# Layer 1's MLP: a plain second half that reads its operand from DRAM, and eight products of the first half ahead of the rest

## The chip, the cores and the metric

One Trainium2 chip, one core. The metric is the device time of one execution of the whole program in microseconds (us), the median of several runs. The names of the engines are those of the profile: PE (TensorE, matrix products), DVE (VectorE), ACT (ScalarE), POOL (GpSimd), SP (the queue that issues the transfers).

## What is computed

A backbone of two layers on 1024 latent tokens of width 1024, with 256 context tokens beside them in layer 0. In each layer a mixer (attention) with an output projection is followed by an MLP. The change concerns the end of layer 1, where only the 1024 latent tokens are left:

```
x   = x + g1 * rms_norm(m, norm_g[1, 1])                    # m: output projection of the mixer
h   = modulate(rms_norm(x, norm_g[1, 2]), sh2, sc2)         # 1024 x 1024
f   = square(relu(h @ w_mlp_in[1])) @ w_mlp_out[1]          # 1024 x 4096, then back to 1024 x 1024
out = x + g2 * rms_norm(f, norm_g[1, 3])
```

All data are float32. A product of two float32 matrices is made of three passes: each operand is split into a high part (rounded to the matrix engine's type) and a low part (the rest), and `dense` (L384 to L391) issues high x high, high x low and low x high into one accumulator, on lines L389, L390 and L391.

## The kernel before, in words

**Splitting.** `split` (L193) copies the high part on ACT (L189) or DVE (L191) and subtracts on DVE or POOL (L196). The split operands live in slots of 128 x 1024, handed out by `Slots` (`R`), and named r, s or w in the profile after the pool that they come from. Every weight is loaded through two staging tiles of 512 KB (tag `stg`, `NSTG = 2`, named ws).

**Output projection** (`out_projection`, L1556). Eight tiles of 128 tokens, each 48 matmuls of 128x512. After a tile comes `residual` (gate, add), and one tile later `late`: `norm_T` normalises, transposes on PE (L316), scales into four raw quadrants xq of the tokens (ACT L321, DVE L323), and for tokens of the first half of the sequence splits quadrants at once. For tiles 4 to 7 `Tokens7.after` (L1355) then forms the token combinations in place with four 128x512 operations (L1362 to L1365), on POOL, for tile 7 on DVE.

**First half of the MLP** (`up7`, L1380). The 4096 hidden features are taken in 16 turns of 256. Each turn is a 2x2 block product done with seven block products in place of eight (Strassen's method in Winograd's form): `Seven` (L1312) forms the combinations of the weight blocks on POOL (L1326, tile cm), `Tokens7` those of the tokens. One block product is 4 k-tiles x 3 passes = 12 matmuls of 128x512, so a turn has 84 and the half 1344. Products 1 and 2 use tokens of the first half of the sequence alone and give the first quadrant of the result; products 5, 6, 3, 7 and 4 need tokens of all eight tiles. Products 1, 6, 7 and 4 add up in one accumulator, which is read in between. In the kernel before, the two products of turn 0 that need no later tokens are issued ahead, before the last `late` (`start` = 2, `begun`). Then `Tokens7.split` (L1367) splits the other four token operands, each as two pairs of 128x1024, and the loop runs with weight operands prepared six products ahead. `put` adds, applies relu and square on DVE (L1444, L1445) and stores the result (hr) in a DRAM tensor hT (L1446).

**Second half** (`Down7`, L1462). Also seven products in place of eight. The 32 rows of 128 hidden features are taken in six units of 2, 2, 3, 3, 3 and 3 pairs. `weights` loads two rows of w_mlp_out per pair and forms seven split operands: combinations on POOL (cm, p, L1326), low parts on POOL (L196). `load` fetches a part of hT for 256 tokens (tile hw), and `prep` forms seven combinations of it (ch, L1326) and their split operands (ho, ACT L189 and L196), on DVE, for the last unit on POOL. Each product is then added into the sums acc (DVE L1552; the first ones are copied by ACT, L1550). In all 16 pairs x 4 token pairs x 7 products x 3 passes = 1344 matmuls of 128x512. The first operands are prepared during the last turn of the first half (`freed`, L2068, as each token operand gives back its slots; `last_up`, L2072). In the last unit `finish1` (L2127) does the final norm, gate and residual of each tile of 128 tokens and stores it.

**Order.** The order on each engine and on SP's queue is fixed when the program is compiled, by a scheduler that goes by the order of the source, its own estimate of times, and `tc.high_priority()` where that is given. At run time every engine and SP work in that order.

**A plain product in the same kernel.** Layer 0's MLP (`mlp`, L1217) does both halves without the seven-product method: split operands, `dense`, sums on DVE (L1244).

## Time and profile before

| | us |
|---|---|
| median of 3 runs | 3236.47 (3233.67 to 3236.80) |
| the profiled execution | 3236.59 |
| its span (first to last instruction) | 3234.8 |
| mean granted clock of PE | 0.982 |

The span and all rows below are of the one profiled execution. "PE busy" counts the records of matmuls, which overlap, so a stretch in which PE is busy throughout is read by the distance from one matmul's start to the next. In the table of stretches the columns are the stretch, its length, the busy time of each engine with the number of its instructions, PE's granted clock (1.00 is 2.4 GHz, 0.50 is 1.2 GHz), and the share and rate of the transfers.

### The profile page before, as it was taken

Reading aid. Unit: us, or ns where it says so; the run is one execution under the profiler, and the core shown is the slowest. Engines: PE = TensorE matmul, PEld = TensorE weight load, DVE = VectorE, ACT = ScalarE, POOL = GpSimd, SP = SyncE. Lnnn points to the kernel's source line nnn. Section 1 sums busy time; section 2 is a strip of 40 time slices with the busy share of each in tenths; the row PEclk is TensorE's granted clock in tenths of the full one; section 3 lists DMA queues with packets and bytes.
Section 4 is the critical chain, followed back from the end, with each engine's and each line's share of the span. In section 5 each row is a group of like instructions: output and inputs, shape, how many; then the busy total and the mean of one; then the engine's idle time right before and its main releaser. Section 6 shows DMA issues by size and latency. Waiting matters only on the chain. (4 is left out here: it accounts for less than half of the span.)

```text
span 3234.8 us, 47996 instructions
## 1 busy us (share of the span) xinstructions
PE 3075.3 (95%) x18037; PEld 2538.6 (78%) x18037; DVE 1745.7 (54%) x3361; ACT 1262.9 (39%) x2664; POOL 1252.0 (39%) x1055
## 2 busy tenths in 40 slices
PE   7999999999999999999999999999998999959997
PEld 4778888887887887878888788999886788836775
DVE  4345565798562343343343641157656655568885
ACT  4222577788342111111111341368854333343432
POOL 2356100135452222322323552301346433484778
PEclk8999999999999999999999999999999899989999
DMA  7555212132332222132211354134443333322233
GB/s 251 179 157 160 84 50 60 56 86 92 126 126 91 65 83 79 55 96 66 71 61 37 107 141 114 34 96 117 135 141 103 108 108 110 114 88 85 89 117 114
DMA packets 242240, 327.59 MB, mean 101 GB/s; under 512 B 37496, under 2 KB 166536, under 8 KB 242008
## 3 DMA queue, kind: packets, MB, share of 16 engines
q1 hardware_dynamic: 241784, 324.01, 32.6%
q8 instruction: 142, 2.33, 0.3%
q14 instruction: 90, 0.74, 0.1%
q10 hardware_dynamic: 128, 0.26, 0.0%
q0 software_dynamic: 96, 0.26, 0.0%
HBM read 256.79 MB, written 67.67 MB: 100 GB/s over the span
## 5 line engine op out<-in xcount | busy, mean ns | idle before, releaser
L196 POOL TENSOR_TENSOR r<-ws,r 128x1024 fp32r<-128x1024 f32 (+1 forms) x100 | 231.1, 2323 | 306.3 <-ACT r L189 306.1
L391 PE MATMUL mm<-s,r 128*128 128x512 f32 (+1 forms) x912 | 318.5, 349 | 0.8 <-POOL r L196 0.7
L389 PE MATMUL mm<-s,r 128*128 128x512 f32 (+1 forms) x912 | 318.6, 349 | 0.0
L390 PE MATMUL mm<-s,r 128*128 128x512 f32 (+1 forms) x912 | 318.1, 349 | 0.0
L1244 DVE TENSOR_TENSOR acc<-mm,acc 128x512 f32<-128x512 f32 x300 | 203.7, 687 | 168.1 <-PE mm L391 167.8
L1230 DVE TENSOR_TENSOR hr<-hr 128x512 f32<-128x512 f32 (+1 forms) x96 | 72.6, 756 | 360.6 <-ACT hr L1229 360.6
L189 ACT ACTIVATE r<-ws 128x1024 fp32r<-128x1024 f32 (+1 forms) x107 | 106.8, 999 | 368.7 <-DMA ws<-in_w_mlp_out_dram 190.7
L189 ACT ACTIVATE pt<-tp 128x512 f32<-128x512 f32 (+1 forms) x382 | 204.1, 548 | 47.4 <-PE tp L802 16.6
L389 PE MATMUL mm<-r,r 128*128 128x512 f32 x538 | 213.0, 396 | 1.3 <-DVE r L191 0.9
L391 PE MATMUL mm<-r,r 128*128 128x512 f32 x538 | 210.1, 391 | 0.6 <-POOL r L196 0.6
L390 PE MATMUL mm<-r,r 128*128 128x512 f32 x538 | 209.6, 390 | 0.0
L1229 ACT ACTIVATE hr<-mm 128x512 f32<-128x512 f32 (+1 forms) x96 | 50.2, 523 | 391.1 <-PE mm L391 383.0
L196 POOL TENSOR_TENSOR r<-hr,r 128x512 fp32r<-128x512 f32 (+1 forms) x66 | 84.5, 1280 | 303.9 <-DVE r L191 303.6
L725 ACT ACTIVATE P<-P,nm 128x1280 f32<-128x1280 f32 (+1 forms) x160 | 189.9, 1188 | 18.2 <-DVE P L733 17.3
L391 PEld LDWEIGHTS mm<-s,r 128*128 128x128 f32 x912 | 171.7, 188 | 25.8 <-POOL r L196 1.2
L390 PEld LDWEIGHTS mm<-s,r 128*128 128x128 f32 x912 | 171.8, 188 | 24.8
L389 PEld LDWEIGHTS mm<-s,r 128*128 128x128 f32 x912 | 171.9, 188 | 24.7
L389 PE MATMUL mm<-r,e 128*128 128x512 f32 (+1 forms) x400 | 151.0, 378 | 2.5 <-ACT e L189 1.6
L391 PE MATMUL mm<-r,e 128*128 128x512 f32 (+1 forms) x400 | 150.7, 377 | 1.7 <-POOL e L196 1.0
L390 PE MATMUL mm<-r,e 128*128 128x512 f32 (+1 forms) x400 | 150.3, 376 | 0.2 <-DVE r L196 0.2
L166 POOL TENSOR_SCALAR sbm<-ssb 128x2 f32<-128x2 f32 x20 | 4.0, 199 | 357.7 <-ACT jk L974 357.6
L1326 POOL TENSOR_TENSOR cm<-ws 128x512 f32<-128x512 f32 x46 | 68.5, 1488 | 181.8 <-DMA ws<-in_w_mlp_in_dram 179.2
(367 smaller groups left out, 8785.1 us busy)
## 6 DMA issues: line engine op xcount, KB each, us to landing
wm<-in_w_mod_dram SPq DMA_DIRECT2D x80, 512.0 KB
ws<-in_w_mlp_in_dram SPq DMA_DIRECT2D x64, 512.0 KB
ws<-in_w_mlp_out_dram SPq DMA_DIRECT2D x64, 512.0 KB
q<-qT SPq DMA_DIRECT2D x224, 128.0 KB
ws<-in_w_in_dram SPq DMA_DIRECT2D x36, 512.0 KB
hT<-hr SPq DMA_DIRECT2D x64, 256.0 KB
hw<-hT SPq DMA_DIRECT2D x16, 768.0 KB
xres<-xn SPq DMA_DIRECT2D x18, 512.0 KB
```

Source lines behind the costliest of these rows:

```text
L166: pool.tensor_scalar(m, ss, 1.0 / n, EPS, op0=OP.mult, op1=OP.add)
L189: act.activation(o, i, AF.Copy)
L196: lo_eng.tensor_tensor(lo, src, f(hi), op=OP.subtract)
L389: pe.matmul(pt, sh, mh, start=first and k == 0, stop=False, skip_group_check=free)
L390: pe.matmul(pt, sh, ml, start=False, stop=False, skip_group_check=free)
L391: pe.matmul(pt, sl, mh, start=False, stop=k == n - 1, skip_group_check=free)
L725: act.activation(P, P, AF.Exp, scale=-1.0, bias=self.nm[:, u:u + 1], accum_out=self.sums[:, u:u + 1])
L1229: act.activation(r, pt, AF.Relu)
L1230: dve.tensor_tensor(r, r, r, op=OP.mult)
L1244: dve.tensor_tensor(acc[t][:, s], pt, acc[t][:, s], op=OP.add)
L1326: self.add.tensor_tensor(o, a, b, op=r[1])
```

## The change

Five things change.

1. The second half is a plain product (`Down`): 32 chunks of 128 hidden features, in eleven units of 2 and ten times 3. A chunk is one load of 512 KB of w_mlp_out and one of 512 KB of hT (all 1024 tokens), each split once. For each of 8 token tiles and 2 column halves a unit makes one accumulation of 3 chunks x 3 passes and adds it to acc. That is 32 x 8 x 2 x 3 = 1536 matmuls. Chunks are prepared after the products of the last turn (`freed`), and then after every second token tile.
2. In the first half, products 1 and 2 of turns 0 to 3 (`early` = 4) are issued after the output projection's last tile and before the last `late`. Their weights are loaded for themselves (`prep_early`, 512 KB in rows of 512 bytes). The result of product 1 is kept for each turn (`keep1`), by transfer for turns 2 and 3, and added on DVE to the later sums of these turns.
3. The token operands of products 5, 6, 7 and 4 are split in two goes: for tiles 4 to 6 (384 of 512 tokens) ahead of the last `late`, for tile 7 after it, there with both low parts on DVE.
4. In both layers' output projections the last tile's `residual` and the last `late` are given high priority.
5. One slot of 128 x 1024 is held for `keep1` until turn 3 ends.

```diff
-        def split(self, p):
+        def split(self, p, o, engs):
             raw = self.q[{5: 11, 7: 12, 6: 22, 4: 21}[p]]
             for c, (a, b) in enumerate(self.slots(p)):
-                split(a, b, raw[:, 2 * c:2 * c + 2, :], act, (dve, pool)[c])
+                split(a[:, :, o], b[:, :, o], raw[:, 2 * c:2 * c + 2, o], act, engs[c])
...
-        seq = [(u, p) for u in range(n) for p in (TURN if u else (1, 2, 5, 6, 3, 7, 4))]
+        seq = [(u, p) for u in range(n) for p in (TURN if u >= early else (5, 6, 3, 7, 4))]
...
+        def prep_early(u):
+            w = stg.tile([128, 1024], F32, tag="stg", name="ws", bufs=NSTG).rearrange("p (a n) -> p a n", a=8)
+            sp.dma_start(w, w_mlp_in[l, :, u * 256:u * 256 + 128].rearrange("(a p) f -> p a f", p=128))
+            for kh in range(2):
+                operand((u, kh + 1), w[:, 4 * kh:4 * kh + 4, :], (dve, pool)[kh])
...
-        ready(start)
+        prep_early(0)
         yield
-        ps, st = env["ps"], {}
-        begun = [product(*x) for x in seq[:start]]
+        ps = env["ps"]
+        keep1 = [x for a in rows() for x in a]
+        for u in range(early):
+            b = product(u, 1)
+            own = keep1[u] if u < 2 else env["mid"].tile([128, 512], F32, tag="O", name="O", bufs=2)
+            act.activation(own, b, AF.Copy)
+            if u >= 2:
+                sp.dma_start(keep1[u], own)
+            if u + 1 < early:
+                prep_early(u + 1)
+            b = product(u, 2)
+            r = env["mid"].tile([128, 512], F32, tag="O", name="O", bufs=2)
+            dve.tensor_tensor(r, b, own, op=OP.add)
+            act.activation(r, r, AF.Relu)
+            pool.tensor_tensor(r, r, r, op=OP.mult)
+            store(u, 0, 0, r)
+        for p in (5, 6, 7, 4):
+            X.split(p, slice(0, 384), (dve, pool))
         yield
...
+                if u < early:
+                    dve.tensor_tensor(st[u, name], b, keep1[u], op=OP.add)
+                else:
+                    act.activation(st[u, name], b, AF.Copy)
...
-                put(1, 0, None)
-
-    class Down7:
...
+                put(1, 0, keep1[u] if u < early else None)
+                if u == early - 1:
+                    env["done1"]()
+
+    class Down:
...
+        def load(self, where):
...
+            w = stg.tile([128, 1024], F32, tag="stg", name="ws", bufs=NSTG)
+            sp.dma_start(w, w_mlp_out[self.l, r, :])
+            h = where.tile([128, 1024], F32, tag="hw", name="hw", bufs=3)
+            sp.dma_start(h, self.hT[r, :])
+            self.raw.append((w, h))
+
+        def prep(self, where):
...
+            s = [R.get(1) for _ in range(4)]
+            v = [x.view([128, 1024]) for x in s]
+            split(v[0], v[1], h, act, dve)
+            split(v[2], v[3], w, act, pool)
+            self.ops.append((s, v[:2], v[2:]))
+            self.load(where)
+
+        def run(self, acc, ps, hp, finish, before_last):
+            for ui, m in enumerate(self.units):
...
+                for t in range(8):
+                    o = slice(t * 128, (t + 1) * 128)
+                    for h in range(2):
+                        s = slice(h * 512, (h + 1) * 512)
+                        pt = ps.tile([128, 512], F32, name="mm", tag="mm", bufs=6)
+                        dense(pt, [(x[0][:, o], x[1][:, o]) for _, x, _ in ops],
+                              [(y[0][:, s], y[1][:, s]) for _, _, y in ops])
+                        if ui == 0:
+                            act.activation(acc[t][:, s], pt, AF.Copy)
+                        else:
+                            dve.tensor_tensor(acc[t][:, s], pt, acc[t][:, s], op=OP.add)
+                    if last:
+                        finish(t, acc[t])
+                    elif t % 2 == 1 and len(self.ops) < self.units[ui + 1]:
+                        self.prep(hp)
...
-            residual(pts, G, xt, xn, ps, pool if i < n - RD else dve)
+            with tc.high_priority() if i == n - 1 else ExitStack():
+                residual(pts, G, xt, xn, ps, pool if i < n - RD else dve)
...
-        late()
+        with tc.high_priority():
+            late()
...
-    D1 = Down7(1, UNITS1, 4, hT)
+    D1 = Down(1, (2,) + (3,) * 10, hT)
...
     for p in (5, 6, 7, 4):
-        X3.split(p)
+        X3.split(p, slice(384, 512), (dve, dve))
...
-    D1.weights(7, temp_down)
-    D1.run(acc, ps, tmp, hp[0], temp_down, 4, finish1, last1)
+    D1.run(acc, ps, hp[0], finish1, last1)
```

## Rows read from the trace of the kernel before

**Rows 1.** The page's head and part 1: span, busy time of each engine.

```profile
span 3234.8 us, 47996 instructions
PE 3075.3 (95%) x18037; PEld 2538.6 (78%) x18037; DVE 1745.7 (54%) x3361; ACT 1262.9 (39%) x2664; POOL 1252.0 (39%) x1055
```

**Rows 2.** Table of stretches: layer 1's MLP in five stretches; last, layer 0's MLP.

```profile
2491.00:2528.40 37.40, 16.41 (x40) 11.47 (x41) 32.06 (x27) 14.19 (x23) 30.85 (x20) 0.59 0.12 39
2528.40:2825.10 296.70, 296.70 (x1288) 241.46 (x1287) 170.44 (x216) 100.97 (x177) 102.94 (x67) 1.00 0.34 114
2825.10:2863.00 37.90, 8.97 (x30) 5.36 (x28) 10.31 (x9) 14.12 (x26) 37.61 (x31) 0.64 0.30 90
2863.00:3223.50 360.50, 322.74 (x1316) 250.03 (x1316) 297.09 (x386) 136.65 (x287) 263.77 (x195) 0.97 0.31 99
3223.50:3234.80 11.30, 0.00 (x1) 0.00 (x0) 5.02 (x8) 1.45 (x4) 3.21 (x3) 0.71 0.41 117
...
1260.00:1680.00 420.00, 420.00 (x2031) 336.96 (x2030) 163.74 (x247) 52.13 (x71) 117.38 (x72) 1.00 0.24 74
```

**Rows 3.** Waits of PE from 2825 to 3226 us: in total, times, longest.

```profile
PE b L389 <- ACT ho L189: 29.4, 4, 26.5
PE a L391 <- DVE ho L196: 13.8, 4, 6.6
PE b L391 <- DVE ho L196: 9.6, 6, 2.7
```

**Rows 4.** Timeline of PE in layer 0's MLP: start, duration, instruction.

```profile
1355.80 0.40 PE L389 MATMUL mm<-s,r 128*128 128x512 f32 x1
...
1364.67 0.40 PE L391 MATMUL mm<-s,r 128*128 128x512 f32 x1
...
1372.63 0.39 PE L389 MATMUL mm<-r,r 128*128 128x512 f32 x1
...
1381.24 0.39 PE L391 MATMUL mm<-r,r 128*128 128x512 f32 x1
```

**Rows 5.** Costliest groups of POOL, DVE and ACT in layer 0's MLP.

```profile
L196 POOL TENSOR_TENSOR r<-ws,r 128x1024 fp32r<-128x1024 f32 x52 | 126.3, 2449 | 247.4 <-ACT r L189 247.4
...
L1244 DVE TENSOR_TENSOR acc<-mm,acc 128x512 f32<-128x512 f32 x240 | 163.2, 688 | 144.5 <-PE mm L391 144.2
...
L189 ACT ACTIVATE r<-ws 128x1024 fp32r<-128x1024 f32 x52 | 55.2, 1063 | 283.9 <-DMA ws<-in_w_mlp_out_dram 183.2 <-PE mm L391 85.5 <-PE mm L390 15.2
```

**Rows 6.** Chain that ended last: two transfers on it, start and time.

```profile
2812.23 3.58 DMA ws<-in_w_mlp_out_dram
...
3075.69 4.82 DMA hw<-hT
```

**Rows 7.** Timeline of DVE and POOL in the last unit.

```profile
3197.19 3.15 DVE L1169 SCALAR_TENSOR_TENSOR acc<-acc,nrr,s 128x512 f32<-128x512 f32 x2
...
3223.12 0.68 DVE L1166 TENSOR_TENSOR acc<-acc,gate 128x512 f32<-128x512 f32 x1
...
3224.32 1.40 DVE L1169 SCALAR_TENSOR_TENSOR acc<-acc,nrr,s 128x512 f32<-128x512 f32 x2
```

**Rows 8.** Timeline of PE, DVE and POOL after the output projection.

```profile
2488.26 1.03 PE L316 MATMUL tr<-ident,xt 128*128 128x128 f32 x8
...
2499.02 0.89 DVE L1362 TENSOR_TENSOR xq<-xq,xq 128x512 f32<-128x512 f32 x1
...
2508.78 2.83 DVE L196 TENSOR_TENSOR w<-cm,w 128x512 fp32r<-128x512 f32 x1
...
2517.17 0.68 DVE L1365 TENSOR_TENSOR xq<-xq,xq 128x512 f32<-128x512 f32 x1
...
2518.91 0.68 DVE L196 TENSOR_TENSOR w<-cm,w 128x512 fp32r<-128x512 f32 x1
...
2498.10 1.27 POOL L1326 TENSOR_TENSOR cm<-ws 128x512 f32<-128x512 f32 x1
...
2507.74 3.32 POOL L196 TENSOR_TENSOR r<-xq,r 128x1024 fp32r<-128x1024 f32 x1
```

More of the change, by code (lines that the diff above doesn't have):

```diff
@@ L32 @@
 BTL = 11 * RPW + 32 + 4 * RPW + 16
-UNITS1 = (2, 2, 3, 3, 3, 3)
 NR = 12
@@ L1378, in free, with up7, operand @@
                     x.free()
-    def up7(l, X, env, hT, ahead, start, freed, last):
+    def up7(l, X, env, hT, ahead, early, rows, freed, last):
         n = FF // 256
-        seq = [(u, p) for u in range(n) for p in (TURN if u else (1, 2, 5, 6, 3, 7, 4))]
-        ops, W, done = {}, {}, [0]
+        seq = [(u, p) for u in range(n) for p in (TURN if u >= early else (5, 6, 3, 7, 4))]
+        ops, W, done, st = {}, {}, [0], {}
+        def operand(key, src, lo):
+            s = R.get(0)
+            v = s.view([128, 2, 4, 128])
+            split(v[:, 0], v[:, 1], src, act, lo)
+            ops[key] = s, [(v[:, 0, k, :], v[:, 1, k, :]) for k in range(4)]
         def prep(u, p):
@@ L1397, in prep @@
                              .rearrange("p (a n) -> p a n", a=4), pool)
-            s = R.get(0)
-            v = s.view([128, 2, 4, 128])
-            split(v[:, 0], v[:, 1], W[u].get(p), act, dve)
-            ops[u, p] = s, [(v[:, 0, k, :], v[:, 1, k, :]) for k in range(4)]
+            operand((u, p), W[u].get(p), dve)
+        def prep_early(u):
[3 more added lines that the diff above has]
+                operand((u, kh + 1), w[:, 4 * kh:4 * kh + 4, :], (dve, pool)[kh])
         def ready(i):
@@ L1408, in product @@
         def product(u, p):
-            k = {1: "b", 2: "a", 5: "c"}.get(p)
+            k = {1: "b", 2: "a", 5: "c"}.get(p, "b" if p == 6 and u < early else None)
             if k:
@@ L1416, in product, with store @@
             return b
-        ready(start)
+        def store(u, fh, th, r):
+            sp.dma_start(hT[u * 256 + fh * 128:u * 256 + (fh + 1) * 128, th * 512:(th + 1) * 512], r)
+        prep_early(0)
         yield
-        ps, st = env["ps"], {}
-        begun = [product(*x) for x in seq[:start]]
+        ps = env["ps"]
[16 more added lines that the diff above has]
+            X.split(p, slice(0, 384), (dve, pool))
         yield
@@ L1427, in up7 @@
             ready(len(seq) if u == n - 1 else i + ahead)
-            b = begun[i] if i < start else product(u, p)
+            b = product(u, p)
             if u == n - 1:
@@ L1445, in put @@
                     dve.scalar_tensor_tensor(r, t, 0.0, t, op0=OP.max, op1=OP.mult)
-                sp.dma_start(hT[u * 256 + fh * 128:u * 256 + (fh + 1) * 128, th * 512:(th + 1) * 512], r)
+                store(u, fh, th, r)
             if p == 1:
@@ L2054, in hybrid_dit_kernel, with rows1 @@
     X3 = Tokens7(xs.enter_context(tc.tile_pool(name="xraw", bufs=1, side="right", reuse_waits="tile")))
-    D1 = Down7(1, UNITS1, 4, hT)
+    D1 = Down(1, (2,) + (3,) * 10, hT)
     env = {"ps": ps}
-    n7, hp = [0], []
-    def temp_up():
-        return env["tmp"].tile([128, 512], F32, tag="cm", name="cm", bufs=3)
-    def temp_down():
-        n7[0] += 1
-        where, tag = ((tmp, "cm"), (hp[0], "p5"), (hp[0], "p6"))[n7[0] % 3]
-        return where.tile([128, 512], F32, tag=tag, name=tag, bufs=1)
+    hp, kept = [], []
+    def rows1():
+        a = stg.tile([128, 2, 512], F32, tag="bg", name="p1", bufs=1)
+        kept.append(R.get(0))
+        b = f(kept[0].view([128, 2, 512]))
+        return [[x[:, h, :] for h in range(2)] for x in (a, b)]
     def freed(p):
-        n7[0] += 1
-        D1.weights((4, 4, 4, 4, 4, 1, 0)[n7[0] - 1], temp_up)
+        D1.prep(hp[0])
     def last_up():
-        for j in range(2):
-            D1.load(0, j, hp[0])
-    first_up = up7(1, X3, env, hT, 6, 2, freed, last_up)
+        for _ in range(2):
+            D1.load(hp[0])
+    env["done1"] = lambda: kept[0].free()
+    first_up = up7(1, X3, env, hT, 6, 4, rows1, freed, last_up)
     with tc.tile_pool(name="t4", bufs=1, reuse_waits="tile") as tmp:
```

102 lines of the change are left out of this document (19 added, 83 removed).

## The prediction

> **What bounds the kernel now.** The head of the page comes first: PE has work for 3075.3 us of a span of 3234.8 us [rows 1]. An average of 95% hides where the rest goes, so the second view is the table of stretches around the change [rows 2]. The reader is to see three kinds of stretch. From 2528.4 to 2825.1 us, the loop of the first half, PE is busy for all of its 296.70 us at the full clock of 2.4 GHz (1.00): 1288 matmuls, 0.2304 us from start to start. Before it, from 2491.0 to 2528.4, PE has 32 matmuls and 8 transposes, which at that pace and by [rows 8] take 7.4 + 1.0 = 8.4 us; the stretch lasts 37.4, so 29.0 us are lost there, with DVE busy for 32.06 and POOL for 30.85. After it, the second half lasts 37.9 + 360.5 = 398.4 us for 1344 matmuls, which would take 309.6 us: 88.8 us are lost. There DVE is busy for 297.09 of 360.5 us and, in the first 37.9, POOL for 37.61.
>
> The third view is PE's waits in the second half [rows 3]: ACT's high parts ho (29.4 us, one wait of 26.5), DVE's low parts ho (13.8 and 9.6). ACT itself is busy for only 136.65 us of this stretch; DVE and POOL, which make the combinations that it copies, are the full ones [rows 2]. So the second half is not bound by PE but by the making of its seven-product operands, and the clock falls where PE waits (0.64 in the first stretch).
>
> For comparison the last row of [rows 2]: layer 0's MLP, plain products, 420 us out of 420 busy, at 1.00.
>
> **The second half.** Removed are all combinations ch, cm and p, seven operands per block, and 1344 matmuls. Added are 1536 matmuls, 192 more. Their pace: [rows 4] show 38 steps in 8.61 us (0.2266) for one pair of slots and 38 in 8.87 us (0.2334) for another; the first half, on mixed slots, has 0.2304. The new operands lie in mixed slots too, so I take 0.2304: 353.9 us, with ends of 348.1 and 358.5.
>
> By the Trainium skill, page "TensorE: Matmul & The Clock Gate", section "Wait — 56ns, not 53.3ns?", back-to-back matmuls of 512 columns start 215.7 ns apart when the clock is full; as an estimate from that, 1536 would take 331.3 us and the sum below would be 22.6 us lower. The rows do not agree: none of them is under 0.2266 us.
>
> What must hide beside it, per unit of three chunks (144 matmuls, 33.2 us): on DVE 16 sums of 0.688 [rows 5] and three low parts of hT, each 128x1024 and so at most two of the 0.68 in [rows 8], together 11.0 + 4.1 = 15.1 us; on ACT six high parts of 1.063, 6.4 us; on POOL three low parts of 2.449, 7.3 us [rows 5]; in transfers three times 3.58 for the weights and at most 4.82 for hT (that row is of 768 KB, the new load of 512 KB) [rows 6], 25.2 us even one after another. All fit into 33.2 us, so I cost them at nothing; what would be late next is the transfers. SP's queue holds little else in this stretch.
>
> The start: a turn of the first half is 84 matmuls, 19.4 us. Two chunks are asked for at its beginning and prepared when products 1 and 2 of this turn give back their slots, after 2.8 and 5.5 us. One chunk needs 3.58 + 2 x 1.063 + 2.449 = 8.2 us [rows 5, 6]. So there is time for two; a new wait here costs between 0 and 8.2 us. I take 1.5, near the lower end, since the change of accumulators is all that is left to wait for. SP's transfers wait there for the staging tiles; queued behind them are the last stores of hT, and behind those DVE's next results. With two result tiles that is covered for about a product or two.
>
> The last unit: per token tile PE needs 18 x 0.2304 = 4.15 us. DVE needs two sums (1.38), one gate product (0.68) and a pair of final operations, 1.40 us when POOL is quiet and 3.15 when it is not [rows 7]: 3.46 to 5.21 us. Over eight tiles the lag is 0 to 8.5 us. POOL no longer makes operands there, so I take 3, the lower half. The end after the last matmul (11.30 us [rows 2]) stays.
>
> Sum: 353.9 + 1.5 + 3 = 358.4 against 398.4: **40.0 us gained**, with ends of 50.3 (348.1 and no wait) and 23.2 (358.5 + 8.2 + 8.5).
>
> **The eight products ahead.** Two of them are ahead now. The other six, 72 matmuls or 16.6 us, move from the full loop into the stretch in which 29.0 us are lost. This is the first term: 16.6 us, if PE finds them ready there. The second is the chain of tile 7: its four combinations on DVE begin at 2499.02 and end at 2517.17 + 0.68 = 2517.85 [rows 8], 18.8 us for work of some 3, because low parts stand between them. High priority brings them together, and three quarters of the splitting needs no tile 7. Against that stands added work on the two engines that are full there: POOL gets four squares and four low parts, eight of 1.27 us, 10.2 us; DVE three more sums and two more low parts, five of 0.68, 3.4 us [rows 8]. The added waits are a chain of product, sum, relu on ACT, square on POOL, store on SP; behind the store on SP are the next early weights, and behind the relu on ACT the high parts of the tokens. Ends: all 29.0 us regained, or 16.6 - 13.6 = 3.0. I take 16.6: what priority gains and what the added work costs I let cancel, since DVE and POOL were each busy for over 80% of this stretch.
>
> **The rest.** In turns 0 to 3 two copies per turn move from ACT to DVE, 8 x 0.68 = 5.4 us, and 2 MB more are loaded; DVE has 126 us free in the 296.7 of the loop, so this costs nothing, and 5.4 us if that cover were gone. Products 1 and 2 of these turns leave the loop with their preparation. One slot fewer leaves six operands in rotation, as many as are asked for ahead. The priority in layer 0 has no row here; I take 0, between 1.0 us gained and lost (a group of eight transposes [rows 8]).
>
> The profiled execution took 3236.59 us, 0.1 from the median. 3236.6 - 40.0 - 16.6 = **3180 us**.
>
> **Rivals.**
> *Blocked engines.* When POOL works, DVE's operations on SBUF stretch: the same low part of 128x512 takes 0.68 us at 2518.91 and 2.83 at 2508.78, while POOL has one of 3.32 [rows 8]. If all the added work on DVE and POOL lies in series with tile 7's chain, 13.6 of the 16.6 us are given back: 3236.6 - 40.0 - 3.0 = 3193.6 us. For it speaks the load of both engines; against it that half of the added work comes before tile 7 is there. The Trainium skill, page "SBUF — State Buffer", section "Who interferes with whom", has such a rule: a DVE instruction with two inputs in SBUF and a POOL instruction that reads SBUF lock each other out for a whole instruction. By that rule, the trace agrees (0.68 against 2.83 us).
> *The fill does not come ahead.* The order is fixed at compile time; if the six products or their weights end up behind tile 7's transposes, they fill nothing: 3196.6 us. Against it: two products do come ahead now.
> *Slower: the staging tiles.* Only two tiles stage weights, and a load for chunk c+2 waits for POOL's low part of chunk c. One chunk in full series is 3.58 + 4.82 + 2.13 + 2.45 = 13.0 us; with two in flight that is 6.5 us per chunk, where PE takes 11.1. It decides once the cycle exceeds 22.2 us, by later preparation or slower transfers. At 26 us, 1.9 us for each of 30 chunks eat 57 us, the whole gain; at 28 us the time is 3180 + 30 x 2.9 = 3267 us. Against it: the transfers of [rows 6].
>
> **Chances and range.** A measurement of this kernel can tell about 0.2% (6.5 us) from no change. My forecast 0.66; blocked engines 0.16; no fill 0.10; slower by staging 0.05; a gain that stalls in the units eat up without more 0.03. So faster 0.92, same 0.03, slower 0.05. The range: downwards the fast pace and no waits, 3180 - 10.3, and half of the remaining 12.4 us of the lost stretch, about 3163; upwards the case without fill and some 8 us of waits in the second half, 3204.
>
> **What would show it.** Right: in the second half PE busy throughout at clock 1.00, 1536 matmuls in 350 to 362 us, DVE under half busy; no wait over 3 us between the halves; 96 matmuls between the output projection's last one and the first product 5; the four combinations of tile 7 side by side. Wrong: a wait of PE for a high or low part at a unit's start that comes back every 33 us (staging); combinations of tile 7 still spread, and DVE operations over 2 us beside POOL (blocked); the six products after tile 7's transposes (no fill); DVE's sums as PE's releaser in the last unit (lag).

## The result, and the profile after

| | before | after |
|---|---|---|
| median of 4 runs each, us | 3235.07 (3233.60 to 3236.80) | 3204.00 (3202.78 to 3210.08) |
| profiled execution, its span | 3236.59, 3234.8 | 3204.88, 3203.1 |
| after / before | 1 | 0.9908, 95% interval 0.9890 to 0.9925 |

31 us of the 56.6 that were forecast; 3204.0 is the upper end of the stated range, which was reckoned for another case (no fill, and 8 us of waits). The page's head and part 1 of the kernel after, beside [rows 1]:

```profile
span 3203.1 us, 47748 instructions
PE 3097.0 (97%) x18229; PEld 2570.5 (80%) x18229; DVE 1624.2 (51%) x3193; ACT 1187.9 (37%) x2448; POOL 1046.6 (33%) x875
```

PE has 192 matmuls more, and yet the span is shorter. The table of stretches of the kernel after, with the columns and stages of [rows 2], shows where:

```profile
2491.00:2528.40 37.40, 19.05 (x81) 14.42 (x80) 31.00 (x36) 18.29 (x35) 30.87 (x22) 0.80 0.28 94
2528.40:2824.40 296.00, 291.97 (x1245) 235.51 (x1245) 180.26 (x218) 96.05 (x157) 103.10 (x65) 0.98 0.38 124
2824.40:2863.00 38.60, 31.92 (x129) 25.38 (x128) 12.77 (x12) 17.18 (x25) 12.91 (x5) 0.91 0.49 153
2863.00:3186.80 323.80, 323.80 (x1411) 264.32 (x1409) 157.87 (x202) 55.56 (x72) 79.08 (x37) 1.00 0.28 93
3186.80:3203.10 16.30, 0.18 (x1) 0.00 (x0) 7.56 (x12) 2.17 (x6) 2.95 (x3) 0.59 0.42 101
```

The fourth row is what the forecast said of the second half: PE busy throughout, at 1.00, 1411 matmuls in 323.80 us (0.2295 each), DVE busy for 49%. In the first row 41 instructions more than in [rows 2] stand in the lost stretch, so the fill did come ahead; but the loop, which had no gap before, now ends only 0.7 us earlier and PE is not busy throughout in it. PE's waits from 2470 us to the end (in total, times, longest):

```profile
PE mm L388 <- ACT w L188: 18.0, 2, 14.4
PE mm L388 <- ACT acc L1541: 5.4, 1, 5.4
PE mm L390 <- DVE w L195: 2.0, 2, 1.4
```

By three milestones of the profiled executions (first matmul of the output projection, last of the first half, last of the second half) the parts are:

| us | before | after |
|---|---|---|
| output projection and first half | 441.33 | 441.33 |
| second half | 397.96 | 362.25 |
| after the last matmul | 11.70 | 16.52 |

The whole gain is the second half's, 35.7 us less 4.8 at the end. The first part of the change, for which 16.6 us were forecast, gave nothing in this trace. Each of these rows is one execution, and kernels with the same source in a stretch differ there: five with this first half, one of them without the priority, have 435.1 to 442.2 us in it (table further below), and the first half of before has 441.3 and 439.4 in two. So a few us of difference in one row prove little by themselves.

**The new wait of 14.4 us.** PE's timeline around it:

```profile
2510.88 0.40 PE L390 MATMUL mm<-s,w 128*128 128x512 f32 x1
2525.72 0.80 PE L388 MATMUL mm<-s,w 128*128 128x512 f32 x1 [14.44 <-ACT w L188]
```

At 2510.88 the last of the 96 matmuls of the eight products ahead starts; the next product starts 14.8 us later. What ran meanwhile, from the chain that ended last (start, duration, what), and below it ACT's timeline:

```profile
2515.68 1.72 POOL O L1447
2517.42 1.99 DMA hT<-O
2519.45 1.87 issue
2521.36 1.04 POOL O L1447
2522.42 2.00 DMA hT<-O
```

```profile
2520.65 0.63 ACT L1446 ACTIVATE O<-O 128x512 f32<-128x512 f32 x1 [1.22 <-DVE O L1445]
2524.52 0.63 ACT L188 ACTIVATE w<-ws 128x512 fp32r<-128x512 f32 x1 [3.24 <-DMA hT<-O]
```

Two early results go out one after the other (square, store; the next sum needs the tile of the one before). Then ACT's first high part of the loop's weights waits for the last store. It does not read hT: the slots of the loop's weights are taken from a pool that lies in the memory of the output projection's temporary pool, and there the early results (tag O) live (the run with a pool of its own, below, shows it). Tile 7's combinations meanwhile, on DVE's timeline:

```profile
2507.45 1.75 DVE L1361 TENSOR_TENSOR xq<-xq,xq 128x512 f32<-128x512 f32 x1
2509.23 2.23 DVE L1362 TENSOR_TENSOR xq<-xq,xq 128x512 f32<-128x512 f32 x1
2516.42 1.52 DVE L1363 TENSOR_TENSOR xq<-xq,xq 128x512 f32<-128x512 f32 x1
2517.98 0.69 DVE L1364 TENSOR_TENSOR xq<-xq,xq 128x512 f32<-128x512 f32 x1
```

They end at 2518.67, no earlier than before (2517.85 [rows 8]), and are still spread and stretched. Seen from tile 7's transposes they end after 20.1 us in place of 22.1, but the transposes come 3.7 us later after the output projection's first matmul.

### The profile page after: what moved, and what is told of

It is laid out like the page before. It is cut to its first block, busy times and chain, and to the rows that moved or that the text cites. A ratio compares the mean times of both kernels' runs of the same rounds, so it can differ in the third digit from the quotient of the medians.

```text
span 3203.1 us, 47748 instructions
## 1 busy us (share of the span) xinstructions
PE 3097.0 (97%) x18229; PEld 2570.5 (80%) x18229; DVE 1624.2 (51%) x3193; ACT 1187.9 (37%) x2448; POOL 1046.6 (33%) x875
## 5 line engine op out<-in xcount | busy, mean ns | idle before, releaser
L195 POOL TENSOR_TENSOR r<-ws,r 128x1024 fp32r<-128x1024 f32 x95 | 233.7, 2472 | 368.1 <-ACT r L188 368.0
L1243 DVE TENSOR_TENSOR acc<-mm,acc 128x512 f32<-128x512 f32 x300 | 203.8, 688 | 168.0 <-PE mm L390 167.7
L388 PE MATMUL mm<-r,r 128*128 128x512 f32 x714 | 281.6, 394 | 0.7 <-DVE r L190 0.7
L390 PE MATMUL mm<-r,r 128*128 128x512 f32 x714 | 279.4, 391 | 0.6 <-POOL r L195 0.6
L389 PE MATMUL mm<-r,r 128*128 128x512 f32 x714 | 277.8, 389 | 0.0
L188 ACT ACTIVATE r<-ws 128x1024 fp32r<-128x1024 f32 x102 | 108.4, 1064 | 379.4 <-DMA ws<-in_w_mlp_out_dram 227.0
L388 PE MATMUL mm<-s,s 128*128 128x512 f32 (+1 forms) x632 | 223.2, 353 | 6.7 <-ACT acc L1541 5.4
L390 PE MATMUL mm<-s,s 128*128 128x512 f32 (+1 forms) x632 | 224.2, 355 | 0.2 <-POOL s L195 0.2
L389 PE MATMUL mm<-s,s 128*128 128x512 f32 (+1 forms) x632 | 223.2, 353 | 0.0
L389 PEld LDWEIGHTS mm<-s,r 128*128 128x128 f32 x912 | 171.5, 188 | 24.9
L1543 DVE TENSOR_TENSOR acc<-mm,acc 128x512 f32<-128x512 f32 x160 | 108.7, 688 | 143.0 <-PE mm L390 143.0
L195 POOL TENSOR_TENSOR s<-ws,s 128x1024 fp32r<-128x1024 f32 x35 | 94.7, 2718 | 245.3 <-ACT s L188 245.3
```

What stands on the lines that cost most here:

```text
L188: act.activation(o, i, AF.Copy)
L195: lo_eng.tensor_tensor(lo, src, f(hi), op=OP.subtract)
L388: pe.matmul(pt, sh, mh, start=first and k == 0, stop=False, skip_group_check=free)
L389: pe.matmul(pt, sh, ml, start=False, stop=False, skip_group_check=free)
L390: pe.matmul(pt, sl, mh, start=False, stop=k == n - 1, skip_group_check=free)
L1243: dve.tensor_tensor(acc[t][:, s], pt, acc[t][:, s], op=OP.add)
```

## The experiments

"First half" and "second half" are the milestones' stretches of the profiled execution, as above; "start" is the distance from tile 7's transposes to the first of the loop's products (27.1 us in the kernel after). A ratio is always to the kernel before, with its 95% interval. Line numbers in rows are those of each kernel, which lie within a few of each other.

### The two parts apart

The first has the new second half with the first half, the output projection and the split of the kernel before; the second has it the other way round.

```diff
-    first_up = up7(1, X3, env, hT, 6, 4, rows1, freed, last_up)
+    first_up = up7(1, X3, env, hT, 6, 2, freed, last_up)
```

> The plain second half alone; first half, output projection and token splitting as in the kernel before. The first half of the changed kernel ended 0.8 us earlier than before, the second half is 35.7 us shorter and the end after the last matmul 4.8 us longer. If the two parts are independent, this kernel has all but 0.8 us of the change: about 3204 us against 3235. If the early products are what lets the second half start well (their stores or slots), it is slower than that, 3210 or more; if they get in its way, faster, 3200 or less.

3202.28 us, 0.9892 (0.9878 to 0.9907); second half 364.5 us. Within the noise that is the time of the kernel after, as expected for independent parts.

```diff
-    D1 = Down(1, (2,) + (3,) * 10, hT)
+    D1 = Down7(1, UNITS1, 4, hT)
```

> The eight products ahead, the split in two goes and the priorities alone; the second half with seven products as before. Theory: the fill is taken back by a new wait of 14.4 us ahead of turn 0's other products and one of 3.6 us in turn 1, so about 3234 us, within 3 us of before. Rival: the part is good for its 16.6 us and the second half's new start took it back, then about 3218 us.

3233.83 us (ten runs), 0.9991 (0.9981 to 1.0000): the theory's 3234, and not the rival's 3218. Its waits of PE have the new one too, with the second half of before:

```profile
PE mm L389 <- ACT w L189: 14.9, 3, 14.5
```

So the second half alone makes the result, and the first part of the change is worth 0 to 6 us of time, with the middle at 2.9.

### Priority

```diff
-        with tc.high_priority():
-            late()
+        late()
```

(and likewise for the last `residual`, in both layers)

> The changed kernel without the high priority of the last residual and the last late, in both layers. If priority is what brings tile 7's four combinations together and forward, the other products start 3 to 8 us later, 3207 to 3212 us. If it mainly pushes the early results' sums back in DVE's order, their last store ends earlier and the time falls, 3199 us or less.

3203.42 us, 0.9897 (0.9879 to 0.9914), with the same wait of 14.4 us. Neither expected outcome came: tile 7's combinations, the early sums and their stores stand where they stood, within 0.02 us of their distance from tile 7's transposes. The priority does nothing that can be measured.

### What the wait of 14.4 us is made of

Tiles of their own for the kept products of turns 2 and 3, so that a result needn't wait for a kept product's transfer:

```diff
-env["mid"].tile([128, 512], F32, tag="O", name="O", bufs=2)
+env["mid"].tile([128, 512], F32, tag="own", name="own", bufs=2)
```

> The changed kernel, with two tiles of their own for the kept product 1 of turns 2 and 3, so that the result of turn 3 no longer waits for the store of turn 2's. Theory (the 14.4 us wait is the chain of the early results, whose tiles must be stored before the first weights' slots of the next pool, in the same memory, may be written): the last store ends some 3 to 5 us earlier than 2524.4, and the first product after the wait starts by as much earlier, about 3200 us. Rival (DVE and POOL are overloaded and block each other, tile 7's operands come late): start unchanged at 2525 or so, 3204 us.

3201.10 us, 0.9899 (0.9876 to 0.9921); the times alone don't tell it from the kernel after. In the trace the theory came: counted from tile 7's transposes the last early store is issued at 20.3 us in place of 23.8, and the start is at 23.6 in place of 27.1, earlier by the same 3.5 us. The wait is 10.9 us.

Product 2 added in the matrix engine onto product 1's accumulator, so that DVE has no early sums (with the tiles above, and with the next turn's product 1 ahead of product 2; of the edit only the part after product 2 is shown):

```diff
-            dve.tensor_tensor(r, b, own, op=OP.add)
-            act.activation(r, r, AF.Relu)
+            act.activation(r, b, AF.Relu)
```

> The changed kernel with the kept tiles of the run on result tiles, and product 2 of an early turn added in product 1's accumulator after ACT has copied it, so that DVE has no early sum; the products of turn u+1 start before product 2 of turn u. Theory (DVE takes the early sums late, in its fixed order behind tile 7's work, and the store and release of their memory hold back the first weights): the last early store ends by 2518 in place of 2524.4, the other products start by 2519, 5 to 8 us gained, 3196 to 3199 us. Rival (tile 7's operands are not ready before 2523 either): 3201 us or more.

3201.68 us, 0.9890 (0.9874 to 0.9905); two waits of 7.0 and 7.9 us, start at 26.0, the last store at 22.7 in place of 20.3. The theory missed. What left DVE came back as a wait on ACT's queue: the copy that frees the accumulator and the last relu stand there behind high parts of tile 7.

Half the turns ahead:

```diff
-    first_up = up7(1, X3, env, hT, 6, 4, rows1, freed, last_up)
+    first_up = up7(1, X3, env, hT, 6, 2, rows1, freed, last_up)
```

> The changed kernel with two turns ahead in place of four: four products, 48 matmuls or 11.1 us fewer in the fill, and no kept result goes by transfer. Theory (the first other product waits for the last early result's sum, square and store): that end comes some 8 to 12 us earlier, the loop is 11.1 us longer, the time within 4 us of 3204. Rival (the wait is for tile 7's own operands): start as before at 2525 or so, 3213 us or more.

3199.91 us, 0.9887 (0.9871 to 0.9902). One wait of 21.4 us, start at 22.5; first half 437.6 us, 3.7 less than in the kernel after, though within what kernels with four turns show (435.1 to 442.2). The time came out as the theory had it, its reason didn't: the last early store is now issued 6.4 us after the transposes, 17 us earlier, and the start is only 4.6 us earlier. In the chain that ended last DVE stands in its place, here in its timeline with two pairs of low parts ahead of tile 7's third combination (which starts at 2518.14):

```profile
2509.77 3.43 DVE L195 TENSOR_TENSOR s<-xq,s 128x256 fp32r<-128x256 f32 x2
2513.12 3.42 DVE L195 TENSOR_TENSOR r<-xq,r 128x256 fp32r<-128x256 f32 x2
```

The early results in a small pool of their own that stays open, so that no slot of the loop lies in their memory (the later results of the first half use the same two tiles):

```diff
...
+    env["mid"] = wp.enter_context(tc.tile_pool(name="mid", bufs=1, reuse_waits="tile"))
     with tc.tile_pool(name="t4", bufs=1, reuse_waits="tile") as tmp:
...
-        env["mid"] = tmp
```

> The early results and the two kept products go to a small pool of their own (4 KB) that stays open, so nothing of the next pools lies in their memory; the later results of the first half use the same two tiles, so that the sum of the memory stays. All else is as in the changed kernel. Theory (memory handed over): the wait of 14.4 us before the first of the other products is the wait of the next pools for the last early store (ends at 2524.4 in the changed kernel's trace). Without it the first weights wait for no store, the first of the other products starts at 2513 to 2519 on that scale, that is 14 to 20 us after tile 7's transposes and not 27, and the time falls by 5 to 10 us. Rival (the engines at the end of the fill): the combinations of tile 7 and the early sums and relus, which are through at 2518 to 2521, end the wait by themselves; the first of the other products then still starts 22 to 27 us after the transposes and the time falls by less than 4 us.

3202.94 us, 0.9897 (0.9881 to 0.9914): by the times alone not to be told from the kernel after. In the trace the start comes at 24.0, 3.1 us earlier, and the first half is 436.1 us. ACT's timeline shows what ends the wait now:

```profile
2521.36 0.72 ACT L188 ACTIVATE r<-xq 128x256 fp32r<-128x256 f32 x2 [2.62 <-DVE xq L1364]
2521.99 1.13 ACT L188 ACTIVATE w<-cm 128x512 fp32r<-128x512 f32 x2
2524.37 0.63 ACT L1446 ACTIVATE hr<-hr 128x512 f32<-128x512 f32 x1 [1.25 <-DVE hr L1445]
```

The last early relu is no longer ahead of the weights (2524.37 after 2521.99); the weights wait in ACT's queue behind tile 7's high part, and that for DVE's last combination. So the memory was the last link of the chain, worth 3 us of the start (27.1 to 27.2 in the five traces with the first half of the kernel after), and right behind it stood the engines. The rival was right there. The first half's 436.1 shows no gain by itself: in those five it is 435.1 to 442.2.

### Amount or order of the work at the end of the fill

In the kernel with the pool of its own, the four early sums, relus and squares left out:

```diff
-            dve.tensor_tensor(r, b, own, op=OP.add)
-            act.activation(r, r, AF.Relu)
-            pool.tensor_tensor(r, r, r, op=OP.mult)
-            store(u, 0, 0, r)
+            store(u, 0, 0, own)
```

> As the kernel with a pool of its own for the early results, four turns ahead, but of the four early results the sum on VectorE, the relu on ScalarE and the square on GpSimd are left out (the first product's copy is stored in their place), so four rows of blocks of the MLP's middle are not the reference's. TensorE's products, the weights, the loads and the stores stay. It takes about 2.7 us from VectorE, 2.5 us from ScalarE and 6.6 us from GpSimd, all between 2490 and 2528. Theory (the engines at the end of the fill are full, and what is done ahead adds to them): the first of the other products starts earlier, 17 to 21 us after tile 7's transposes in place of 24.0, and the first half becomes 3 to 6 us shorter. Rival (the order on the queues and the late weight loads set the wait, not the amount of work): the first of the other products starts 23 to 24 us after the transposes as before, and the time moves by less than 2 us.

3198.93 us, 0.9884 (0.9867 to 0.9900); start at 22.0, between the two expectations, and first half 436.3, no shorter. Two stretches of each trace explain it: 41 us from 8 us ahead of tile 7's transposes, and the rest of the first half. First the kernel after, then the one with the pool of its own, then this one:

```profile
2490.58:2531.58 41.00, 22.66 (x91) 17.23 (x91) 33.45 (x38) 19.34 (x37) 32.05 (x23) 0.79 0.32 107
2531.58:2824.56 292.98, 288.95 (x1237) 233.16 (x1236) 178.38 (x216) 95.42 (x156) 102.31 (x64) 0.99 0.38 123
```

```profile
2490.63:2531.63 41.00, 25.21 (x97) 19.16 (x97) 36.78 (x39) 19.11 (x37) 34.51 (x24) 0.79 0.33 112
2531.63:2819.34 287.71, 284.63 (x1231) 230.37 (x1230) 176.60 (x215) 95.45 (x156) 100.74 (x64) 1.00 0.37 125
```

```profile
2490.53:2531.53 41.00, 28.76 (x118) 22.15 (x118) 34.98 (x40) 18.81 (x36) 32.64 (x22) 0.88 0.33 108
2531.53:2819.83 288.30, 282.55 (x1212) 227.82 (x1211) 177.01 (x214) 94.01 (x154) 98.72 (x62) 0.99 0.37 124
```

With less work PE gets 21 instructions more into the stretch (97 to 118; 4.8 us at 0.2304), as the theory had it. But the rest of the first half is no shorter with 19 fewer: PE loses there what it gained (9.3 us in place of 4.3). The table below has this for all.

The other test changes the order alone: no token operand is split before tile 7's combinations, each whole behind them. Once from the best kernel (below), with two turns ahead, once with four:

```diff
-        for p in (5, 6, 7, 4):
-            X.split(p, slice(0, 384), (dve, pool))
...
-        X3.split(p, slice(384, 512), (dve, dve))
+        X3.split(p, slice(0, 512), (dve, pool))
```

> The kernel with two turns ahead, the pool of its own and the first unit's copies on VectorE (3189.0, first of the other products 12.4 us after tile 7's transposes, first half 435.1 us), but no part of the token products 5, 6, 7 and 4 is split before tile 7's combinations: each is split whole behind them, in the order in which the products come, low parts in turn on VectorE and GpSimd. The amount of work stays, its order changes. Theory (order): tile 7's combinations stand side by side within 8 us after the transposes, product 5 starts at 10 to 12 us and the others follow, and the first half becomes 3 us or more shorter. Rival (amount: VectorE and GpSimd are full for 22 us, whatever comes first): the combinations come early but the products then crawl behind the low parts, and the first half is as long or longer, 435 to 440 us.

3193.81 us, 0.9868 (0.9851 to 0.9884), 4.8 us over the best kernel; first half 438.3 in place of 435.1. The combinations do stand early and product 5 starts 4.7 us after the transposes, but then PE stops three times more, 6.3, 6.6 and 3.5 us from start to start, and the rival's lengthening came.

> The same order with four turns ahead: the kernel with the pool of its own (first half 436.1 us, start 24.0 us after the transposes), copies of the first unit on VectorE, and the token products split whole behind tile 7's combinations. Theory (order): the first of the other products starts 8 us earlier or more, and with 96 products ahead the first half comes to 428 to 432 us. Rival (amount): products 5, 6, 7 and 4 start one by one behind their low parts, and the first half stays at 434 to 438 us.

3191.48 us, 0.9864 (0.9849 to 0.9878); start at 18.4, 5.6 us earlier, and the first half 436.1 all the same, to the tenth what the other order gave (the copies on DVE, below, are the rest of the gain). DVE's timeline:

```profile
2501.41 1.77 DVE L1361 TENSOR_TENSOR xq<-xq,xq 128x512 f32<-128x512 f32 x1
...
2511.18 2.82 DVE L1364 TENSOR_TENSOR xq<-xq,xq 128x512 f32<-128x512 f32 x1
```

The combinations are through at 2514.0 and not at 2521.3, and it does not help: the splitting of these operands all stands behind them now, and PE waits 9.6 us for a high part of the weights on ACT and 5.9 us for a low part on DVE. So with four turns the other order brings 8 matmuls more into the 41 us (96 in place of 88) and less work 21 (109); in neither is the first half shorter, because the loop loses 6.2 and 9.3 us. In the fill the amount counts for more than the order; for the whole first half neither test shows a gain.

In the best kernel, two casts of tile 7 moved from DVE to ACT:

```diff
-            split(hi, lo, v[:, k0:k0 + n, :], dve, lo_engs[h])
+            split(hi, lo, v[:, k0:k0 + n, :], getattr(parts, "hi", dve), lo_engs[h])
...
+            if i == 7:
+                parts.hi = act
```

> The kernel with two turns ahead, the pool of its own and the first unit's copies on VectorE (3189.0), and the two high-part casts of tile 7, 1.25 and 0.81 us on VectorE there, moved to ScalarE, which idles beside them. Theory (VectorE's work at the end of the fill sets the start): tile 7's combinations come up to 2 us earlier and the time falls by 1 to 2 us, 3187 to 3188. Rival (the wait is GpSimd's and the queues' order): no change, 3188.5 to 3190.

3189.74 us, 0.9852 (0.9838 to 0.9867): no change against 3188.97. The start does come 2.0 us earlier, 10.4 in place of 12.4, as the theory had it, but the first half is 436.2: PE waits for the products behind it instead.

One turn ahead:

```diff
-    first_up = up7(1, X3, env, hT, 6, 4, rows1, freed, last_up)
+    first_up = up7(1, X3, env, hT, 6, 1, rows1, freed, last_up)
```

> One turn ahead (as many products ahead as in the kernel before), the pool of its own and the copies of the first unit on VectorE. If products done ahead are worth their pace (12 matmuls each, 2.8 us), the first half is 24 x 0.23 = 5.5 us longer than with two turns ahead (435.1 us). Rival (what is done ahead is given back at the end of the fill, because VectorE and GpSimd set the start of the others): 434 to 437 us, the same as with two or four turns.

3194.34 us, 0.9871 (0.9857 to 0.9886), 5.4 us over two turns; first half 439.7, 4.6 longer than with two turns and close to the 5.5 that 24 matmuls take. So the second turn ahead is worth nearly its pace, and the third and fourth, in these kernels, nothing (435.1 with two, 436.1 with four).

From PE's timeline of each profiled execution (512-column matmuls only; the 41 us are those from 8 us ahead of tile 7's transposes; "lost" is the stretch less 0.2304 us for each matmul):

| kernel | turns ahead | matmuls in the 41 us | rest of the first half: matmuls, lost us | first half us |
|---|---|---|---|---|
| before | two products | 43 | 1286, 0.1 | 441.3 |
| after | 4 | 82 | 1235, 8.2 | 441.3 |
| after, first copies on DVE | 4 | 81 | 1236, 8.8 | 442.2 |
| after, no priority | 4 | 82 | 1235, 6.3 | 439.5 |
| first part alone | 4 | 81 | 1236, 3.9 | 437.3 |
| after, scale of the final norm on ACT | 4 | 81 | 1236, 1.6 | 435.1 |
| pool of its own | 4 | 88 | 1229, 4.3 | 436.1 |
| the same, less work | 4 | 109 | 1210, 9.3 | 436.3 |
| the same, other order | 4 | 96 | 1221, 6.2 | 436.1 |
| pool of its own | 2 | 76 | 1248, 0.8 | 435.1 |
| pool of its own | 1 | 57 | 1268, 0.8 | 439.7 |

With four turns ahead the loop itself loses 3.9 to 9.3 us in all these kernels but one, with one or two turns 0.8. In the kernel after most of this is one wait, ahead of the loop's 14th product; the chain that ended last shows its cause, and two 6-us stretches show what follows (the row above them is from the start after the 14.4 us):

```profile
2560.01 5.02 DMA ws<-in_w_mlp_in_dram
2565.19 1.26 POOL cm L1325
```

```profile
2524.00:2530.00 6.00, 3.71 (x8) 2.52 (x9) 4.67 (x5) 2.93 (x5) 3.88 (x3) 0.50 0.28 86
...
2566.00:2572.00 6.00, 2.88 (x6) 1.87 (x7) 3.51 (x5) 2.41 (x4) 4.26 (x4) 0.70 0.02 8
2572.00:2578.00 6.00, 6.00 (x20) 4.69 (x20) 3.36 (x6) 0.00 (x0) 0.00 (x0) 0.73 0.51 175
```

A load of weights is late, PE waits 3.6 us until 2569.0, and the granted clock is 0.70 and 0.73 in the two stretches around it, so partly 1.2 GHz: in the 9.0 us from then on 26 matmuls start where 39 would. A turn whose products 1 and 2 are done has 60 matmuls left, 13.8 us in place of 19.4, and needs the same two loads and combinations of weights. But that alone does not make the wait: the kernel with the scale of the final norm on ACT has the same source in the first half, and it has no such wait (0.4 us in its loop) and loses 1.6 us. What differs is the order that the scheduler gave the engines and SP there. SP's timeline of the kernel after with one row of POOL's, under it the same of the other:

```profile
2543.92 0.34 SPq L1512 DMA_DIRECT2D hw<-hT  x1
2544.36 0.38 SPq L1398 DMA_DIRECT2D ws<-in_w_mlp_in_dram  x1
...
2549.78 1.28 POOL L1325 TENSOR_TENSOR cm<-ws 128x512 f32<-128x512 f32 x1 [10.42 <-DMA ws<-in_w_mlp_in_dram]
...
2555.85 0.38 SPq L1398 DMA_DIRECT2D ws<-in_w_mlp_in_dram  x1
...
2560.01 0.38 SPq L1398 DMA_DIRECT2D ws<-in_w_mlp_in_dram  x1
```

```profile
2546.69 0.37 SPq L1399 DMA_DIRECT2D ws<-in_w_mlp_in_dram  x1
...
2550.43 1.29 POOL L1326 TENSOR_TENSOR cm<-ws 128x512 f32<-128x512 f32 x1 [7.00 <-DMA ws<-in_w_mlp_in_dram]
...
2556.49 0.38 SPq L1399 DMA_DIRECT2D ws<-in_w_mlp_in_dram  x1
...
2561.24 0.38 SPq L1399 DMA_DIRECT2D ws<-in_w_mlp_in_dram  x1
```

From the loop's first product (2525.72 and 2529.74) the three loads are issued after 18.6, 30.1 and 34.3 us in the one, after 17.0, 26.8 and 31.5 in the other. In the kernel after, a load of the second half's operand (hw) stands ahead of the first of them and waits on SP for a store of hT to land, 3.0 us. Issued 0.4 us behind that load, the weights are there for POOL after 5.4 us, in the other kernel after 3.7. The next load can only follow when POOL's combinations give back the staging tile (2555.83), so it is 3.3 us later too. In all eight four-turn kernels with the hw load ahead of the weights PE waits for late weights in the loop, 2.6 to 4.4 us; the first part alone has it behind them too, and no wait over 1.1 us. With one turn or two the hw load stands ahead in most kernels as well, and no such wait follows. So it went with both, short turns and the load ahead in SP's queue. That these are the cause was not tried by itself.

### The start and the end of the second half

ACT's timeline at the beginning of the second half of the kernel after:

```profile
2838.36 1.06 ACT L188 ACTIVATE r<-ws 128x1024 fp32r<-128x1024 f32 x1 [6.23 <-DMA ws<-in_w_mlp_out_dram]
2839.32 3.02 ACT L1541 ACTIVATE acc<-mm 128x512 f32<-128x512 f32 x6
```

The first unit's sums are copied by ACT, and the six copies stand behind a high part that waits 6.2 us for a load. The accumulators stay full, and PE waits (5.4 us). With the copies on DVE:

```diff
-                            act.activation(acc[t][:, s], pt, AF.Copy)
+                            dve.tensor_copy(acc[t][:, s], pt)
```

> The changed kernel, with the first unit's 16 copies into the sums on DVE in place of ACT. Theory (PE's wait of 5.5 us at 2834 comes from ACT's queue: the copies stand behind a high part that waits 6.2 us for a late weight load): the wait goes, and with it the matmuls at half clock behind it, 6 to 8 us, about 3197 us. Rival (the chunks themselves come late, the next unit waits instead): under 2 us gained, 3202 or more.

3197.45 us, 0.9880 (0.9865 to 0.9894); second half 354.99 us, 7.3 less, as the theory had it. Over all traces the plain second half takes 358.2 to 364.5 us with the copies on ACT (nine kernels) and 354.3 to 355.6 with them on DVE (six). Its first 38.6 us in this kernel:

```profile
2829.30:2867.90 38.60, 36.84 (x160) 29.64 (x159) 24.42 (x31) 8.53 (x9) 13.58 (x5) 1.00 0.53 177
```

160 matmuls at 1.00 where the kernel after has 129 at 0.91. The wait of 5.4 us had cost about 7.3, with the clock.

At the end, the last unit's final operations: DVE's timeline, and POOL's beside the second row:

```profile
3160.96 1.40 DVE L1168 SCALAR_TENSOR_TENSOR acc<-acc,nrr,s 128x512 f32<-128x512 f32 x2
...
3174.40 2.44 DVE L1168 SCALAR_TENSOR_TENSOR acc<-acc,nrr,s 128x512 f32<-128x512 f32 x2 [0.44 <-POOL nrr L183]
```

```profile
3174.34 1.29 POOL L1165 TENSOR_TENSOR acc<-acc,gate 128x512 f32<-128x512 f32 x1
```

From 3174 on POOL's gate product of the next tile starts at the same moment as DVE's pair, which takes 2.44 us and not 1.40; four pairs in a row come 5.14 us apart, where PE needs 4.15 for a tile. To take the scale off DVE:

```diff
-                dve.scalar_tensor_tensor(dst[:, s], dst[:, s], r, xt[:, s], op0=OP.mult, op1=OP.add)
+                act.activation(dst[:, s], dst[:, s], AF.Copy, scale=r)
+                (dve if h else pool).tensor_tensor(dst[:, s], dst[:, s], xt[:, s], op=OP.add)
```

> The changed kernel; in the final norm the scaling by the root goes to ACT and the residual is added by POOL for the first column half and DVE for the second, in place of two combined operations on DVE. Theory (in the last unit DVE needs 5.1 us per token tile where PE needs 4.1, so it is behind at the end): DVE falls to about 3.0 us per tile, the time after the last matmul from 16.5 us to 12 or 13, about 3200 us. Rival (the end is the chain of the last tile alone): the chain gets one step longer, 3204 to 3206 us.

3200.15 us, 0.9886 (0.9870 to 0.9902), but after the last matmul 16.3 us pass as before (16.5). The gain is in the first half of that run (435.1 us), whose source the edit does not touch: there the scheduler's order differs, and the wait in the loop is gone, as shown above. In its trace one addition still takes 1.60 us on DVE beside POOL's, and the last tile's norm now waits for ACT and for that addition. A miss. The other kernels with the plain second half, whose last unit no edit touches, end 14.6 to 16.5 us after the last matmul, so that 16.5 isn't a firm price either.

### The edits together

The pool of its own, two turns ahead, the first copies on DVE:

> Three edits together: the early results in a pool of their own as above, two turns ahead in place of four, and the copies of the second half's first unit on VectorE. Theory: the edits act in different places, so that their gains add up: about 4 us for two turns (3200 alone), about 6 us for the copies (3197.5 alone) and what the pool of its own gives; 3188 to 3194, with no wait over 12 us at the end of the fill and none in the second half's first units. Rival: two turns ahead and the pool of its own are two ways to the same few us, so that their sum is that of one: 3193 to 3197.

3188.97 us (3188.46 to 3190.27), 0.9851 (0.9837 to 0.9866): 15 us under the kernel after, and the best; the rival's 3193 to 3197 did not come. Alone the three edits gave 1.1, 4.1 and 6.6 us, so they add up or a little more, as the theory had it: first half 435.1, second half 355.0, end 14.6 us. The longest wait at the end of the fill is 11.3 us.

## Why the prediction was wrong, point by point

**The eight products ahead: the step that failed.** The prediction said of the six further ones "I take 16.6: what priority gains and what the added work costs I let cancel". Measured were 0.0 us between the milestones, and 2.9 (0 to 6) for this part alone. Only a part of the step held: 39 more matmuls (82 in place of 43, 9.0 us) lie in the stretch that had been lost. What failed is the cancelling. Priority gained nothing, and behind the work ahead the loop's first product starts only 27.1 us after tile 7's transposes. And two costs were on no side of the sum: the store of the last early result, for which the next pool's memory waits (3 us of the start), and the late weights in the loop with the clock behind them (8.2 us lost in the rest of the first half, 0.1 before). With 0.9 us more lost ahead of the stretch, that is the whole 9.0. The chain of product, sum, relu, square and store had been written out; what was not asked is who takes over the tile at its end, and "this costs nothing", said of the loop's loads by DVE's free time, left out the place of these loads in SP's queue. The second of these costs isn't fixed: with another order from the scheduler the same first half lost 1.6 us there and took 6.3 us less.

The rival of the blocked engines (3193.6, chance 0.16) was the nearest in kind, and its sign in the trace came: combinations spread, DVE's operations over 2 us beside POOL. On those, by the Trainium skill, page "SBUF — State Buffer", section "Who interferes with whom", an operation of DVE with two inputs in SBUF and one of POOL that reads SBUF shut each other out for a whole instruction; the trace agrees at the end too (2.44 for a pair beside POOL's 1.29, 1.40 without). That this rival left 3.0 of the 16.6 us and the part alone gave 2.9 is partly luck, for in the kernel after most was lost in the loop and not in tile 7's chain. The rival that the fill does not come ahead fell, though its time (3196.6) lay closer than the forecast.

**The second half** was right in kind: 35.7 us less, 40.0 forecast. The pace was 0.2295 (0.2304 taken), all 1536 matmuls run, DVE is half idle, no wait comes back by the unit: the staging rival fell. The term of the start was too small: 1.5 taken, ends 0 to 8.2, and 6.9 more than that by the milestones (362.25 against 353.9 + 1.5). The prediction looked for the wait at the operands; it was the copies of the sums in ACT's queue behind an operand that waited for its load. Moving them gave 7.3 back. In the other kernels with the copies on ACT the excess over 355.4 is 2.8 to 9.1 us.

**The last unit:** 3 us of lag taken, ends 0 to 8.5; the end after the last matmul grew by 4.8, in most other kernels by about 3, so the term was about right. The reason why POOL would be quiet there (no operands) was true and yet not enough: POOL's gate product of the final norm meets DVE's pair.

**The rest** at nothing: the two copies per turn on DVE did not show as a wait; the loop was not free all the same, for its loads (above).

Of the 24.9 us missing between 56.6 forecast and 31.7 in the profiled executions, the fill is 16.6, the start of the second half 6.9 and the lag 1.8, which is all of it to half a microsecond.

## What to carry to other kernels

Work that fills a gap of PE is worth its pace only as far as the engines that end the gap have room for what it adds: here the second turn ahead brought 4.6 us, the third and fourth nothing, and doing the splitting in another order brought nothing either. When a chain of temporaries ends in a store, ask which pool takes over its memory and who waits there; and keep what empties the accumulators off a queue on which operands wait for loads. Moving work out of a loop also shortens the time in which the loop's loads must arrive; whether they then came late went here with what stood ahead of them in SP's queue, so look at that queue's order in the trace, also where the source is the same.

## Not expected of the hardware

The clock makes short waits dearer than they are: around and after PE's wait of 3.6 us in the loop the granted clock was 0.70 to 0.73 over 12 us, and a third of the matmuls was missing in the 9 us after the wait; after the 14.4 us it was 0.50 (1.2 GHz) until 2530, 8 matmuls from 2525.7 on where 18 would have started. In the second half's start 5.4 us of waiting cost about 7.3.
